# Letting an accumulating DMA make the lo part of every second weight chunk in the middle of a decoder layer's down projection

## The chip, the cores and the metric

The kernel runs on one core of one Trainium2 chip. Four engines compute: TensorE (PE in the profile; its weight loads are PEld), VectorE (DVE), ScalarE (ACT) and GpSimd (POOL). SyncE (SP) issues DMAs. Each engine works through its own queue in order and waits on semaphores for the others; transfers run on 16 DMA engines. The metric is the device time of one execution in microseconds, the median of several runs.

## The reference, cut to what matters

One decoder layer in float32, for 256 tokens of width 2048: a projection, two groups of attention heads, an output projection, a layer norm, a feed-forward block with a short convolution, and a second layer norm.

```python
D_MODEL = 2048; SEQ = 256; FFN_DIM = 5632
proj = h @ w_in[l]
a_out = diff_attention(q_d, k_d, v_d, lam, lam_init, subln_g[l], cos_d, sin_d)
b_out = moba_attention(q_m, k_m, v_m, cos_m, sin_m)
mix = jnp.concatenate([a_out, b_out], axis=-1) @ w_out[l]
h = layer_norm(DEEPNORM_ALPHA * h + mix, ln1_g[l], ln1_b[l])
f = conv_ffn(h, w_up[l], conv_w[l], conv_b[l], w_down[l])
h = layer_norm(DEEPNORM_ALPHA * h + f, ln2_g[l], ln2_b[l])

def conv_ffn(h, w_up, conv_w, conv_b, w_down):
    u = h @ w_up
    g, val = u[..., :FFN_DIM], u[..., FFN_DIM:]
    gp = jnp.pad(g, ((0, 0), (CONV_W - 1, 0), (0, 0)))
    gc = conv_b + sum(conv_w[j] * gp[:, j:j + S] for j in range(CONV_W))
    return (jax.nn.silu(gc) * val) @ w_down
```

The change lies in the last product, `(silu(gc) * val) @ w_down`, [256 tokens x 5632] by [5632 x 2048].

## The kernel before, in words

All weights pass through the core once, as a stream of chunks of 128 partitions x 2048 columns of float32 (1 MB): `v`, `q`, `k` chunks for the attention, 16 `o` chunks, 88 `g` and `u` chunks for the up projection, and 44 `d` chunks for the down projection, one for each 128 rows of `w_down`. In what follows a `d` chunk is counted from 0 to 43 (`i - first_d` in the code).

TensorE multiplies in a rounded format, float32r. To keep float32's precision, each operand is split into a hi part (the value rounded to float32r) and a lo part (the value minus hi, rounded too), and a product is made of three: hi by hi, hi by lo, lo by hi. `split(i, half)` does this for half a chunk: ScalarE copies 128 x 1024 columns of the loaded tile `raw` into `hi` (L122), and VectorE subtracts `hi` from `raw` into `lo` (L123). `hi` and `lo` come from a pool of six buffers each, that is three chunks; `raw` from a pool of four.

The program is written out step by step, one step for each chunk, and the order in which it is written is the order of every engine's queue. At the start of step i `begin(i)` puts down the split of the activations of chunk i + 2 (`split_act`, L447 on ScalarE and L448 on VectorE, in the down projection), the split of the second half of chunk i + 2, and the load of chunk i + 6 (L105, on SP's queue). In the middle of the step `middle(i)` puts down the split of the first half of chunk i + 3. So chunk i's load is put down six steps ahead, its first half is split 2.5 steps ahead and its second half two.

In the down projection the tokens stand still and the weights move. A step has 24 matmuls of 128 x 512 columns (`mm_d`, `mm_token`, L190): first columns 0 to 1023, for both halves of the tokens, then columns 1024 to 2047. For each pair of banks the order is hi by hi, twice, hi activations by lo weights, twice, lo activations by hi weights, twice. All eight PSUM banks accumulate over the 44 chunks; the last four chunks are taken out of the loop and finish bank by bank. At step 24 the second layer norm's two vectors are loaded (`load_gb`, L376, 1 MB each). After the last product z is normalised by VectorE, ScalarE and GpSimd and stored.

GpSimd does little: constants, a few powers, and the end of the last layer norm (L771, L772). All DMAs are issued by SP.

Tiles of the pool `keep` with the same tag share their place: tag `t2` holds x2 (the input), then h2 (the normed input of the up projection, in use until it ends), and from step 38 on `ends` (the split parts of the last four chunks).

Of the kernel before, what the change touches and what calls it, by code (L numbers as in the profile page):

```python
# [12 lines left out]
F32R = mybir.dt.float32r  # L13
AF = mybir.ActivationFunctionType
ALU = mybir.AluOpType

P = 128
# [15 lines left out]
LAM_INIT = 0.8 - 0.6 * math.exp(0.0)  # L33
MASKED = -3.0e38

# columns of the pack of per-partition vectors
C_G1, C_B1, C_W, C_CB, C_SG = 0, KT, 2 * KT, 2 * KT + 3 * FT, 2 * KT + 4 * FT
N_COLS = C_SG + 1

# [6 lines left out]
def hymba_layer(ctx: ExitStack, tc: tile.TileContext, a: dict):  # L46
# [13 lines left out]

    bank = [psum.tile([P, 512], F32, name=f"bank{i}") for i in range(8)]

    # ------------------------------------------------------------ weights
    loaded, parts = {}, {}

    stream = []
# [7 lines left out]
        for j in range(8):  # L74
            stream.append(("o", half, j, a["w_o"][half, j]))
    for f in range(FT):
        # the first two hold g and val of the first 128 features together, half of the rows each
        stream.append(("g", f, 0, a["w_u"][f, 0]))
        stream.append(("u", f, 0, a["w_u"][f, 1]))
    for f in range(FT):  # L80
# [4 lines left out]
    first_d = next(i for i, s in enumerate(stream) if s[0] == "d")  # L85

    def pieces(i, half=None):
        """Column ranges in which a chunk is loaded (or one half of it split): short where all else waits for it."""
        if i == 0:
            cuts = [0, 512, 1024, 1536, 2048]  # L90
        elif i < 4:
            cuts = [0, 512, 1024, 1536, 2048] if half is not None or i < 2 else [0, 1024, 2048]
        else:
            cuts = [0, 2048] if half is None else [0, 1024, 2048]
        both = [(x, y) for x, y in zip(cuts, cuts[1:])]
        return [p for p in both if half is None or p[0] // 1024 == half]

    def load(i):
        if i >= NS:
# [6 lines left out]
        loaded[i] = t  # L106

    def split(i, half, both=None):
        """hi and lo parts of half a chunk's columns, in the rotating buffers or in both."""
        if i >= NS or (i, half) in parts:  # L110
            return
        t = loaded[i] if half == 0 else loaded.pop(i)
        if both is None:
            hi = splits.tile([P, 1024], F32R, name="hi")
            lo = splits.tile([P, 1024], F32R, name="lo")
        else:
            hi, lo = both[:, half], both[:, 2 + half]
        for x, y in pieces(i, half):
            if i < 4 and x % 512 == 0:
                split_x(4 * i + x // 512, 4 * i + (y + 511) // 512)  # L120
            s = slice(x - 1024 * half, y - 1024 * half)
            ACT.activation(hi[:, s], t[:, x:y], AF.Copy)  # L122
            DVE.tensor_tensor(lo[:, s], t[:, x:y], hi[:, s].bitcast(F32), ALU.subtract)  # L123
        parts[i, half] = (hi, lo)

    def weights(i, x, w):
        """hi and lo parts of columns x to x + w of chunk i."""
        hi, lo = parts[i, x // 1024]
        return hi[:, x % 1024:x % 1024 + w], lo[:, x % 1024:x % 1024 + w]

    # ------------------------------------------------------------ activations of the layer's input
    # hi and lo parts of a row tile side by side, so that one product takes both
    x2 = keep.tile([P, KT, 2, S], F32R, name="x2", tag="t2")
    xh, xl = x2[:, :, 0], x2[:, :, 1]
    z = keep.tile([P, 2, D], F32, name="z")
# [7 lines left out]
        ACT.activation(xh[:, k0:k1], t, AF.Copy)  # L143
        DVE.tensor_tensor(xl[:, k0:k1], t, xh[:, k0:k1].bitcast(F32), ALU.subtract)

    # ------------------------------------------------------------ constants
    cst = {}

    def load_table(n):
# [21 lines left out]
    def lambdas():  # L171
        vec, lam4 = cst["vec"], cst["lam4"]
        pr = keep.tile([P, 2, SUB], F32, name="pr")
        DVE.tensor_tensor(pr[:, 0], lam4[:, 0], lam4[:, 1], ALU.mult)
        DVE.tensor_tensor(pr[:, 1], lam4[:, 2], lam4[:, 3], ALU.mult)
        ls = keep.tile([P, 4], F32, name="ls")
        DVE.reduce_sum(ls[:, 0:2], pr, axis=mybir.AxisListType.X)
        ACT.activation(ls[:, 2:4], ls[:, 0:2], AF.Exp)
        nlam = keep.tile([P, 2], F32, name="nlam")
        # -lambda = (exp(l2) - exp(l1)) - lambda_init  # L180
        DVE.tensor_tensor(nlam[:, 0:1], ls[:, 3:4], ls[:, 2:3], ALU.subtract)
        DVE.tensor_scalar(nlam[:, 1:2], nlam[:, 0:1], -LAM_INIT, None, op0=ALU.add)
        cst["nlam"] = nlam[:, 1:2]
        sg = keep.tile([P, 1], F32, name="sg")
        DVE.tensor_scalar(sg, vec[:, C_SG:C_SG + 1], 1.0 - LAM_INIT, None, op0=ALU.mult)
        cst["sg"] = sg

    # ------------------------------------------------------------ matrix products
    def mm(out, lhsT, rhs, start, stop):
        PE.matmul(out, lhsT, rhs, start=start, stop=stop)  # L190

    def mm_feature(dst, i, t2):
        """dst, a bank: [128 features, 256 tokens] twice, to be added up; the weights stand still."""
        for k in range(KT):
            if k == KT // 2:
                middle(i)
            wh, wl = weights(i, k * P, P)
            mm(dst, wh, t2[:, k].rearrange("p j t -> p (j t)"), k == 0, False)
            mm(dst[:, 0:S], wl, t2[:, k, 0], False, k == KT - 1)

    def added(dst, src):
        """dst = the sum of a bank's two halves."""
        ACT.activation(dst, src[:, S:2 * S], AF.Copy)
        DVE.tensor_tensor(dst, src[:, 0:S], dst, ALU.add)  # L204

    def mm_token(dst, i, x, ah, al, first, last):
        """dst, banks of [128 tokens, 512 features], from the chunk's columns x and on; the tokens stand still."""
        w = [weights(i, x + c * 512, 512) for c in range(len(dst))]
        for c, d in enumerate(dst):
            mm(d, ah, w[c][0], first, False)  # L210
        for c, d in enumerate(dst):
            mm(d, ah, w[c][1], False, False)
        for c, d in enumerate(dst):
            mm(d, al, w[c][0], False, last)

    # ------------------------------------------------------------ attention
    mh = keep.tile([P, NH, S], F32R, name="mh", tag="ma")
    ml = keep.tile([P, NH, S], F32R, name="ml", tag="mb")
    vals = {}
# [98 lines left out]
        att[h] = pt  # L318

    def mixed(h, scale):  # L320
        """hi and lo parts of a head's output, [head dim, tokens]."""
        scale = cst["sg"] if scale else None
        src = OB[:, S:2 * S]
        hi, lo = mh[:, h], ml[:, h]
        if scale is None:
            ACT.activation(hi, src, AF.Copy)
            DVE.tensor_tensor(lo, src, hi.bitcast(F32), ALU.subtract)
        else:
            ACT.activation(hi, src, AF.Copy, scale=scale)
            DVE.scalar_tensor_tensor(lo, src, scale, hi.bitcast(F32), op0=ALU.mult, op1=ALU.subtract)  # L330
# [34 lines left out]
        mm(OB[:, S:2 * S], v[:, 0, c], pt[:, 0:S], True, False)  # L365
        mm(OB[:, S + P:2 * S], v[:, 1, c], pt[:, S:S + P], False, True)

    # ------------------------------------------------------------ layer norm
    gb = {}
    stats = {}  # L370

# [20 lines left out]
        POOL.tensor_tensor(rstd, ve, cst["half"][:, 0:1], ALU.pow)  # L392
        return mv, rstd

    # ------------------------------------------------------------ feed-forward
    acts = {}

    def act_of(f):
# [21 lines left out]
    gates = {}  # L420

    def gated(f, g):
        """silu of the convolution; g [128 features, tokens]"""
        vec = cst["vec"]
        w = [vec[:, C_W + j * FT + f:C_W + j * FT + f + 1] for j in range(3)]
        gc = work.tile([P, S], F32, name="gc", tag="on")
# [21 lines left out]
        DVE.tensor_tensor(lo, src, hi.bitcast(F32), ALU.subtract)  # L448
        aparts[f] = (hi, lo)

    # ------------------------------------------------------------ the program
    idle = keep.tile([P, 512], mybir.dt.bfloat16, name="idle")
    DVE.memset(idle, 0.0)
    for i in range(4):
        load(i)
    for i in range(WARM):
        # the tensor engine's clock rises while the first loads are on their way
        mm(bank[7], idle[:, 0:P], idle, True, True)
    for i in range(2):
        split(i, 0)  # L460
# [2 lines left out]
    split(2, 0)  # L463

    def begin(i):
        """At the start of step i: what runs ahead of it, and what has waited for step i - 1."""
        urgent(i)
        j = i + 2
        if j < NS and stream[j][0] == "d":
            split_act(stream[j][1])  # L470
        split(j, 1)
        load(i + 6)
        pending(i)

    def middle(i):
        """Halfway through step i, when the first half of its weights is done with."""
        urgent(i + 0.5)
        if i + 3 < NS:
            split(i + 3, 0)
        pending(i + 0.5)  # L480
# [129 lines left out]
        DVE.tensor_tensor(hl[:, 4 * c:4 * c + 4, ts], hf, hi.bitcast(F32), ALU.subtract)  # L610

    def mm_first(t, c):
        """g and val of the first 128 features, [tokens, features], from a quarter of the rows."""
        ts = slice(t * P, (t + 1) * P)
        for kk in range(4):
            k = 4 * c + kk
# [81 lines left out]
    at(first_u + 3, act_out, 0, bank[0][:, S:2 * S])  # L698

    def h_piece(n):  # L700
        """z becomes the layer norm's own output, [tokens, features]."""
        t, c = divmod(n, 4)
        s = slice(c * 512, (c + 1) * 512)
        DVE.tensor_tensor(z[:, t, s], z[:, t, s], gb["g"][:, s], ALU.mult)
# [16 lines left out]
    def mm_d(i, t, cs):  # L721
        f = stream[i][1]
        ah, al = aparts[f]
        ts = slice(t * P, (t + 1) * P)
        # the last 512 columns of the second half of the tokens end in banks of their own
        end = FT - 1 - PAIRED_END if (t, cs) == (1, [3]) else FT - 1
        mm_token([bank[4 * t + c] for c in cs], i, cs[0] * 512, ah[:, ts], al[:, ts], f == 0, f == end)

    def mm_d_end(j):
        """The last chunks' share of half j of the last 512 columns, in a bank of its own."""  # L730
        for i in last:
            wh, wl = weights(i, 1536 + j * 256, 256)
            ah, al = (x[:, P:2 * P] for x in aparts[stream[i][1]])
# [91 lines left out]

# [1 line left out]
def _tables():  # L827
    """Rotary tables, [head dim, tokens], and the causal mask."""
    out = {}
    pos = np.arange(S, dtype=np.float32)  # L830
    for n, width, rot in (("d", SUB, SUB // 4), ("m", HD, HD // 4)):
# [61 lines left out]
```

## Time and profile before

| | |
|---|---|
| time, median of 3 runs | 1148.24 us (1147.97 to 1148.28) |
| span of the profiled execution | 1146.0 us |
| HBM read | 214.80 MB |
| DMA queues' share of 16 engines' span | 53.2% hardware_dynamic, 0.3% and 0.1% instruction |
| instructions | 15269 |

The span runs from the first to the last instruction of one profiled execution; the time of a run has a little more around it. In the page's rows of slices each digit is the busy share of one of 40 equal slices, in tenths. A grouped line reads: line, engine, operation, tiles out<-in, shapes, count | busy time, mean ns of one | idle time of the engine just before, and what ended it. A DMA row reads: tiles, issuing queue, count, KB each, median us from issue to landing.

### The profile page before, as it was taken

Reading aid. Unit: us, or ns where it says so; the run is one execution under the profiler, and the core shown is the slowest. Engines: PE = TensorE matmul, PEld = TensorE weight load, DVE = VectorE, ACT = ScalarE, POOL = GpSimd, SP = SyncE. Lnnn points to the kernel's source line nnn. Section 1 sums busy time; section 2 is a strip of 40 time slices with the busy share of each in tenths; the row PEclk is TensorE's granted clock in tenths of the full one; section 3 lists DMA queues with packets and bytes.
Section 4 is the critical chain, followed back from the end, with each engine's and each line's share of the span. In section 5 each row is a group of like instructions: output and inputs, shape, how many; then the busy total and the mean of one; then the engine's idle time right before and its main releaser. Section 6 shows DMA issues by size and latency. Waiting matters only on the chain.

```text
span 1146.0 us, 15269 instructions
## 1 busy us (share of the span) xinstructions
PE 1132.2 (99%) x5992; PEld 967.8 (84%) x5992; DVE 747.7 (65%) x1183; ACT 570.1 (50%) x895; POOL 20.8 (2%) x27
## 2 busy tenths in 40 slices
PE   9999999999999999999999999999999999999996
PEld 6888888888888898888888888888888888888885
DVE  6895886857745777777656666566666555555566
ACT  6555554544443485454554545455454444444441
POOL 0000000000000000000000000000000000000004
PEclk9999999999999999999999999999999999999998
DMA  9765455455455456555555555555555555556521
GB/s 329 280 220 193 153 179 179 154 182 184 156 178 190 174 219 222 184 187 190 194 201 185 184 188 187 200 193 188 184 184 193 195 192 191 184 210 233 185 106 74
DMA packets 33768, 217.89 MB, mean 190 GB/s; under 512 B 3744, under 2 KB 5664, under 8 KB 8480
## 3 DMA queue, kind: packets, MB, share of 16 engines
q1 hardware_dynamic: 33696, 216.92, 53.2%
q8 instruction: 47, 0.77, 0.3%
q14 instruction: 25, 0.20, 0.1%
HBM read 214.80 MB, written 2.10 MB: 189 GB/s over the span
## 4 chain that ended last, share of the span: by engine, by line
PE 98%; DVE 1%; POOL 1%; DMA 0%; ACT 0%; issue 0%; SPq 0%; POOLq 0%
PE bank L190 97%; PE bank L313 0%; POOL z L772 0%; DMA raw<-in_w_v 0%; POOL z L771 0%; DVE z L780 0%; PE bank L595 0%; PE bank L360 0%; ACT hf L598 0%; DVE h L610 0%; POOL rstd L392 0%; DVE z L822 0%; DVE bank L821 0%; DVE st L384 0%; DVE z L776 0%
## 5 line engine op out<-in xcount | busy, mean ns | idle before, releaser
L123 DVE TENSOR_TENSOR lo<-raw,hi 128x1024 fp32r<-128x1024 f32 (+1 forms) x394 | 468.0, 1202 | 283.8 <-ACT hi L122 283.4
L122 ACT ACTIVATE hi<-raw 128x1024 fp32r<-128x1024 f32 (+1 forms) x394 | 404.3, 1038 | 282.5 <-PE bank L190 252.4
L190 PE MATMUL bank<-h,hi 128*128 128x512 f32 x1376 | 477.2, 390 | 0.0
L190 PE MATMUL bank<-h,lo 128*128 128x256 f32 x1376 | 388.0, 282 | 0.0
L190 PEld LDWEIGHTS bank<-h,hi 128*128 128x128 f32 x1376 | 258.2, 188 | 54.1
L190 PEld LDWEIGHTS bank<-h,lo 128*128 128x128 f32 x1376 | 260.1, 189 | 0.0
L190 PE MATMUL bank<-x,hi 128*128 128x512 f32 x512 | 181.6, 396 | 0.0
L190 PE MATMUL bank<-x,lo 128*128 128x256 f32 x512 | 144.3, 282 | 0.0
L190 PEld LDWEIGHTS bank<-x,hi 128*128 128x128 f32 x512 | 96.1, 188 | 21.7 <-issue 1.3
L190 PE MATMUL bank<-hi,al 128*128 128x512 f32 (+1 forms) x338 | 107.1, 393 | 0.0
L190 PE MATMUL bank<-lo,ah 128*128 128x512 f32 (+1 forms) x338 | 107.1, 393 | 0.0
L190 PE MATMUL bank<-hi,ah 128*128 128x512 f32 (+1 forms) x338 | 107.1, 393 | 0.0
L190 PEld LDWEIGHTS bank<-x,lo 128*128 128x128 f32 x512 | 96.8, 189 | 0.2
L190 PE MATMUL bank<-hi,x 128*128 128x512 f32 x256 | 86.3, 407 | 0.4 <-ACT hi L122 0.4
L190 PEld LDWEIGHTS bank<-hi,al 128*128 128x128 f32 x338 | 63.7, 188 | 14.7
L190 PEld LDWEIGHTS bank<-lo,ah 128*128 128x128 f32 x338 | 63.7, 188 | 14.7
L190 PEld LDWEIGHTS bank<-hi,ah 128*128 128x128 f32 x338 | 63.6, 188 | 14.7
L190 PEld LDWEIGHTS bank<-hi,x 128*128 128x128 f32 x256 | 49.1, 192 | 13.0 <-ACT hi L122 1.3
L427 ACT ACTIVATE gc<-gs,vec 128x256 f32<-128x256 f32 x43 | 25.9, 602 | 58.7 <-DVE gs L204 58.7
L190 PE MATMUL bank<-lo,x 128*128 128x512 f32 x128 | 51.5, 402 | 0.0
L430 ACT ACTIVATE gc<-gc 128x256 f32<-128x256 f32 x44 | 18.4, 418 | 48.9 <-DVE gc L429 48.9
L447 ACT ACTIVATE ah<-act 128x256 fp32r<-128x256 f32 x44 | 18.2, 416 | 49.2 <-DVE lo L123 45.5
(122 smaller groups left out, 828.7 us busy)
## 6 DMA issues: line engine op xcount, KB each, us to landing
raw<-in_w_u SPq DMA_DIRECT2D x88, 1024.0 KB, 4.8
raw<-in_w_d SPq DMA_DIRECT2D x44, 1024.0 KB, 4.8
raw<-in_w_qk SPq DMA_DIRECT2D x32, 1024.0 KB, 4.9
raw<-in_w_o SPq DMA_DIRECT2D x16, 1024.0 KB, 4.8
raw<-in_w_v SPq DMA_DIRECT2D x12, 1024.0 KB, 4.8
raw<-in_w_v SPq DMA_DIRECT2D x8, 256.0 KB, 4.8
raw<-in_w_v SPq DMA_DIRECT2D x4, 512.0 KB, 7.9
z<-in_x SPq DMA_DIRECT2D x1, 2048.0 KB, 9.7
```

Of the source, the lines that this page charges most:

```text
L122: ACT.activation(hi[:, s], t[:, x:y], AF.Copy)
L123: DVE.tensor_tensor(lo[:, s], t[:, x:y], hi[:, s].bitcast(F32), ALU.subtract)
L190: PE.matmul(out, lhsT, rhs, start=start, stop=stop)
L427: ACT.activation(gc, g, AF.Identity, bias=vec[:, C_CB + f:C_CB + f + 1], scale=w[2])
L430: ACT.activation(gc, gc, AF.Silu)
L447: ACT.activation(hi, src, AF.Copy)
```

## The change

For the twelve `d` chunks 8, 10, ..., 30 the splitting is done in another way (`by_dma`, `split_dma`). For each half, ScalarE copies `raw` with scale -1 into lo, so that lo holds minus hi; a DMA from GpSimd's queue adds `raw` to lo in SBUF; and ScalarE copies `raw` into hi as before. VectorE has no part in it. hi and lo lie in one tile, `spare`, of the same place as h2 and `ends` (tag `t2`), with two slots that edited chunks use in turn; the rotating buffers are left to the odd chunks there. All of a chunk's four copies and two DMAs are put down in `begin`, three steps ahead of the chunk, after the second half of the chunk before it has been split and ahead of that step's load. The later calls of `split` for such a chunk find its parts made and return. The loading of `raw`, the matmuls and their order are as before. Comments were taken out of the file, and lines behind the new functions are numbered 18 to 20 higher.

```diff
+    def by_dma(i):
+
+        return first_d + 8 <= i < NS - 12 and (i - first_d) % 2 == 0
+
+    spare = []
+
+    def split_dma(i):
+        if not spare:
+            spare.append(keep.tile([P, 2, 2, 2048], F32R, name="spare", tag="t2"))
+        hi, lo = (spare[0][:, (i - first_d) // 2 % 2, j] for j in range(2))
+        t = loaded.pop(i)
+        for half in range(2):
+            s = slice(1024 * half, 1024 * (half + 1))
+            ACT.activation(lo[:, s], t[:, s], AF.Copy, scale=-1.0)
+            POOL.dma_start(lo[:, s], t[:, s], accum_op=ALU.add)
+            ACT.activation(hi[:, s], t[:, s], AF.Copy)
+            parts[i, half] = (hi[:, s], lo[:, s])
...
     def begin(i):
         urgent(i)
         j = i + 2
         if j < NS and stream[j][0] == "d":
             split_act(stream[j][1])
         split(j, 1)
+        if by_dma(i + 3):
+            split_dma(i + 3)
         load(i + 6)
         pending(i)
```

## The prediction

> **What bounds the kernel now.** I read the profile page first, for the engine that carries the span.
>
> ```profile
> PE 1132.2 (99%) x5992; PEld 967.8 (84%) x5992; DVE 747.7 (65%) x1183; ACT 570.1 (50%) x895; POOL 20.8 (2%) x27
> PE   9999999999999999999999999999999999999996
> PEclk9999999999999999999999999999999999999998
> PE 98%; DVE 1%; POOL 1%; DMA 0%; ACT 0%; issue 0%; SPq 0%; POOLq 0%
> ```
>
> TensorE is busy in every slice but the last, at full granted clock, and the chain that ended last is 98% matmuls. So VectorE at 65% is not a bound, only a helper that must be in time. The edit lies in the down projection, whose steps I marked off in the timeline by the split of the activations, the first ScalarE instruction of a step:
>
> ```profile
> 899.93 0.42 ACT L447 ACTIVATE ah<-act 128x256 fp32r<-128x256 f32 x1 [1.26 <-PE bank L190]
> ...
> 950.12 0.42 ACT L447 ACTIVATE ah<-act 128x256 fp32r<-128x256 f32 x1 [1.26 <-DVE lo L123]
> 950.59 1.06 ACT L122 ACTIVATE hi<-raw 128x1024 fp32r<-128x1024 f32 x1
> 953.38 1.06 ACT L122 ACTIVATE hi<-raw 128x1024 fp32r<-128x1024 f32 x1 [1.73 <-PE bank L190]
> ...
> 955.71 0.42 ACT L447 ACTIVATE ah<-act 128x256 fp32r<-128x256 f32 x1 [1.27 <-DVE lo L123]
> ```
>
> One step takes 5.58 us (955.71 - 950.12, and nine steps since 899.93), one matmul of its 24 so 0.232 us. The first row is the fifth of these splits, so it opens the step of chunk 2, and 950.12 that of chunk 11. The edited stretch, from three steps before chunk 8 to the end of chunk 30, then runs from about 917 to 1062. The windows and the grouped lines of 140 us of it:
>
> ```profile
> 922.00:1062.00 140.00, 140.00 (x604) 113.48 (x604) 72.14 (x76) 63.83 (x76) 0.00 (x0) 1.00 0.57 205
> L190 PE MATMUL bank<-hi,al 128*128 128x512 f32 x202 | 63.3, 394 | 0.0
> L123 DVE TENSOR_TENSOR lo<-raw,hi 128x1024 fp32r<-128x1024 f32 x51 | 62.5, 1225 | 55.6 <-ACT hi L122 55.6
> L122 ACT ACTIVATE hi<-raw 128x1024 fp32r<-128x1024 f32 x50 | 53.1, 1061 | 44.4 <-PE bank L190 43.2
> ```
>
> The columns of the first row are the busy time of PE, weight loads, VectorE, ScalarE and GpSimd, then clock, DMA share and GB/s. PE is busy in all 140 us and its matmuls have 0.0 us of idle time before them. ScalarE waits for matmuls to free buffers, VectorE waits for ScalarE: both are paced by PE. No wait here is left to remove. The resource that the edit newly loads is DMA, at 57%:
>
> ```profile
> DMA  4826646448256465382573643835649988357266
> GB/s 197 281 56 262 206 131 265 133 171 293 66 241 213 117 269 147 157 300 54 248 241 91 267 152 147 300 94 211 236 101 377 426 358 304 87 213 269 54 276 183
> q1 hardware_dynamic: 3920, 28.58, 56.8%
> raw<-in_w_d SPq DMA_DIRECT2D x25, 1024.0 KB, 4.8
> gb<-in_ln_g SPq DMA_DIRECT2D x1, 1024.0 KB, 6.9
> gb<-in_ln_b SPq DMA_DIRECT2D x1, 1024.0 KB, 9.0
> ```
>
> Loads come in bursts with gaps between them; only where the two layer-norm vectors are loaded too does it stay at nine tenths, there at up to 426 GB/s.
>
> **The change, part by part.**
>
> *VectorE.* 24 subtractions leave (12 chunks, two halves): 24 x 1.225 = 29.4 us off VectorE. Worth nothing, since none stands before PE (0.0 idle above). The gain is bounded above by the same zero.
>
> *ScalarE.* 24 copies with scale -1 are added, 24 x 1.061 = 25.5 us, priced as the hi copy of the same shape. ScalarE goes from 63.83 to about 89 of 140 us. They come in a burst: at the start of the step three before an edited chunk j it runs the activation split, hi of the odd chunk, then lo, hi, lo, hi: 0.42 + 5 x 1.06 = 5.7 us, against a step of 5.58. Queued behind is the next activation split, 0.15 us late and due two steps later. Cover: PE's own 5.58 us per step; the margin is some two steps. Cost zero. The edited chunks also leave the rotating hi and lo buffers, so odd chunks wait less for them; that helps nobody who bounds.
>
> *The wait for the spare buffers.* Chunk j overwrites the slot of chunk j - 4, whose last matmul ends just as that step starts. ScalarE is tied to that moment already by the activation split. Cost zero.
>
> *GpSimd.* It issues 24 DMAs and does nothing else in the window (0.00 busy). SP takes this much to issue one, and GpSimd's longest operation in the chain of waits was:
>
> ```profile
> L105 SPq DMA_DIRECT2D raw<-in_w_d x44: 327/328/328, 858.5 to 1097.9; - x44
> 1130.61 1.70 POOL z L771
> ```
>
> Between 0.33 and 1.70 us apiece; I take the longer one. Two issues in two steps (11.15 us) are then 3.4 us, hidden, and only add to the delay of the sum. Behind them on GpSimd's queue stands nothing until the last layer norm.
>
> *The raw buffers.* Until now a load waited for VectorE's subtraction; for the edited chunks it waits for both accumulating DMAs, and SP runs in order, so the odd chunk's load stands behind it.
>
> ```profile
> SPq L105 <- DVE lo L123: 556.7, 103, 25.2
> ```
>
> A load is issued 3.5 steps (19.5 us) before ScalarE's first copy of it and lands in 4.8, so 14.7 us of lateness are free. If the second accumulation, issued 4.7 us into a step, lands like a load, at 9.5, SP's next load goes out some 4 us late, inside that margin.
>
> *The accumulating DMA itself.* No row shows one. Deadlines first. The first lo half is ready for it at 0.42 + 2 x 1.06 = 2.5 us into the step, PE reads it three steps and two matmuls in, at 17.2 us: 14.7 us are allowed. The second is issued at 4.7 and read twelve matmuls later, at 20.0: 15.3 us. Behind a matmul that waits for lo stands all of PE. A whole load lands in 4.8, so a lone accumulation is in time. What matters is the throughput: in every two steps (11.15 us) there are two loads of 1 MB and two accumulations of 512 KB.
>
> Price of a load: 0.568 x 140 / 27.3 chunks of 1.05 MB (28.58 MB) = 2.91 us of all 16 engines in this stage; at the crowded rate, 1.05 MB / 426 GB/s = 2.46 us. One pass over 512 KB is half of it: 1.46 or 1.23 us. Lower bound of an accumulation: one pass, like a copy, 1.23 us. Upper bound: a row is read, added and written back with the time of two loads' landings one after the other, 9.6 us. The ends are far apart. I take three passes, since it fetches raw, fetches the destination and writes the destination, and I see no row that says that they overlap: 3 x 1.46 = 4.4 us, or 3 x 1.23 = 3.7 us at the crowded rate. That is nearest to the row of the 1 MB load of the same tile.
>
> *Sum.* At the stage's own price, two steps need 2 x 4.4 + 2 x 2.91 = 14.6 us of DMA in 11.15: 3.5 us too much, 12 times, 42 us; the two vector loads add 5; some 15 us of lateness are free: +32. At the crowded price, 2 x 3.7 + 2 x 2.46 = 12.3: 1.2 us too much, 14 us, +5 -15: +4. I take the middle, +18, rounded down to +17. On the profiled span, 1146.0 + 17 = 1163; with the 2.2 us that lie outside it (1148.24 - 1146.0), 1165 us.
>
> The collectives bear on this: the Trainium skill, "Collectives: The Full Stack", section "The bandwidth ceiling: the fold count and why AG ≠ RS ≠ AR", says that an add in the DMA path costs nothing itself and only doubles the reads. By it an accumulation would be two passes; no run here shows it. It is the first rival below.
>
> **The rivals.**
>
> *It fits (not slower).* The write-back runs beside the next row's reads, so an accumulation is two passes, 2 x 1.23 = 2.46 us. Two steps then need 4 x 2.46 = 9.8 us, less than 11.15. This case holds below (11.15 - 4.92) / 2 = 3.1 us per accumulation, with the free lateness (15 - 5) / 24 = 0.4 more, 3.5. For it: gaps in the DMA row, and landings with 15 us to spare. Against it: the loads leave gaps because they wait for buffers; they don't show that a read-modify-write streams. Time: 1148.2.
>
> *One at a time (much slower).* Accumulations wait for their own reads, the two landings of 4.8 us, while loads pass between them. A pair takes 19.2 us, 8.05 more than two steps; 12 x 8.05 - 15 = +82: 1230. For it: 256 KB and 1 MB loads land alike, so much of a landing is waiting and not bytes; against it: bursts at 426 GB/s show many packets in flight at once.
>
> ```profile
> raw<-in_w_v SPq DMA_DIRECT2D x8, 256.0 KB, 4.8
> ```
>
> *Faster.* Something I can't see paces matmuls by VectorE's traffic; idle 0.0 and clock 1.00 in the window speak against it. If the 24 subtractions' whole 29.4 us slowed PE by a tenth, it would be -3: 1145.
>
> **How the numbers follow.** Overfilled DMA 50%, own range 1152 to 1180. It fits, 23%. One at a time 17%. Other costs, such as descriptor making on GpSimd longer than 5.6 us apiece or instruction fetches behind crowded queues, 6%, slower. Faster, 4%. A measurement of this kernel tells about 0.2% (2.3 us) from no change. Faster 0.04, same 0.23, slower 0.73. The range from 1147.6 to 1215 holds the fit, the forecast and about half of the slow rival.
>
> **What would show it.** Right: in the edited stretch the DMA row stands at nine tenths throughout, PE gets gaps before matmuls that read the spare tile's lo, released by the accumulating DMA, growing after some four pairs; the window of 140 us becomes about 157, all else keeps its length; VectorE loses 24 instructions, ScalarE gains 24. Wrong: PE keeps 0.0 idle and DMA stays below nine tenths (it fits); or DMA has gaps while PE waits for the accumulation (one at a time); or PE waits for ScalarE's hi, which would void my zero for the burst; or GpSimd's queue is solid with issues.

## The result, and the profile after

The changed kernel takes 1148.99 us (median of 20 runs, 1147.57 to 1150.36) against 1147.57 us of the kernel before on the same chips (20 runs, 1146.48 to 1148.29): a ratio of 1.0014, 95% interval 1.0007 to 1.0020. That is 1.4 us more, within the 0.2% that the prediction called no change. The forecast was 17 us more.

From the page of the changed kernel, the lines that answer to those of before (the lines have moved: L123 is now L141, L190 L208, L105 L123; L111 to L113 are the new copies and the new DMA):

```profile
span 1146.8 us, 15285 instructions
PE 1132.4 (99%) x5992; PEld 967.0 (84%) x5992; DVE 717.6 (63%) x1159; ACT 587.1 (51%) x919; POOL 41.9 (4%) x51
DVE  6895886857745777776666666566666523232566
POOL 0000000000000000000000000000000011110004
DMA  9755455455455456555555555555555589999721
q1 hardware_dynamic: 33696, 216.92, 53.0%
q0 software_dynamic: 3456, 12.58, 5.8%
```

The edit does what it says: VectorE has lost 24 instructions and 30 us, ScalarE has gained 24 instructions, GpSimd has 24 more and shows in four slices where it had nothing. DMA goes from five and six tenths to eight and nine there. TensorE's busy time is the same within 0.2 us.

The windows, the grouped lines and the DMA answer for the same 140 us as before, then the waits of SP's queue over the whole edited stretch (917 to 1062), of the changed kernel:

```profile
922.00:1062.00 140.00, 140.00 (x602) 113.16 (x601) 41.97 (x51) 78.06 (x97) 19.43 (x23) 1.00 0.99 279
L208 PE MATMUL bank<-spare,ah 128*128 128x512 f32 x192 | 52.7, 396 | 0.0
L112 POOL DMA_DIRECT2D spare<-raw x23 | 20.0, 869 | 105.8 <-ACT spare L111 104.7 <-PE bank L208 1.0
...
q1 hardware_dynamic: 3625, 26.42, 51.8%
q0 software_dynamic: 3456, 12.58, 47.1%
raw<-in_w_d SPq DMA_DIRECT2D x24, 1024.0 KB, 9.1
spare<-raw POOLq DMA_DIRECT2D x23, 512.0 KB, 9.5
...
SPq L123 <- DMA spare<-raw: 124.5, 12, 16.3
```

TensorE is busy in all 140 us, and the matmuls that read the accumulated lo have 0.0 us of idle time before them, as before the change. Yet the DMA share went from 0.57 to 0.99, and both kinds of transfer now land 9 to 10 us after their issue. All of the new work fits, by this share only just. Does the backlog grow from pair to pair? Two windows of 22 us (about four steps) of the DMA answer, one early and one with the two layer-norm vectors:

```profile
DMA  8997999989999999999999998999999999999986
GB/s 164 223 231 127 223 201 186 134 104 141 365 343 417 432 417 432 432 402 417 387 432 432 417 402 313 298 283 268 290 298 328 238 246 216 201 201 216 216 171 119
q0 software_dynamic: 562, 2.04, 51.0%
q1 hardware_dynamic: 576, 4.19, 48.9%
raw<-in_w_d SPq DMA_DIRECT2D x4, 1024.0 KB, 8.5
spare<-raw POOLq DMA_DIRECT2D x4, 512.0 KB, 8.6
```

```profile
q1 hardware_dynamic: 676, 5.01, 60.4%
q0 software_dynamic: 514, 1.84, 42.7%
raw<-in_w_d SPq DMA_DIRECT2D x4, 1024.0 KB, 17.1
spare<-raw POOLq DMA_DIRECT2D x4, 512.0 KB, 9.7
gb<-in_ln_g SPq DMA_DIRECT2D x1, 1024.0 KB, 11.2
gb<-in_ln_b SPq DMA_DIRECT2D x1, 1024.0 KB, 13.0
```

The first is 966 to 988: four loads (4.19 MB) and four accumulations land, in 8.5 and 8.6 us. The second is 1032 to 1054: only there do the loads fall behind, to 17.1 us, and they catch up when the edit ends. There is no growth in between (9.3 and 9.5 us for 988 to 1010, 9.1 and 9.4 for 1010 to 1032). Nor does the time shrink that is left between an accumulation's landing and TensorE's first read of it. By the trace it is 4.7 us for the first half of chunk 8, 3.7 for that of chunk 26, and 2.6 at the least up to chunk 28; only for the last one, behind the vectors' loads, is it 0.9 us.

The row of rates in the first window shows two levels. Where accumulations run alone (201 to 216 GB/s, near its end) 512 KB take some 2.5 us, and where loads run alone (417 to 432 GB/s, in its middle) 1 MB takes some 2.5 us too.

So the mechanism to be settled is the price of an accumulation, the time for which it holds all 16 engines. Three theories stood before the experiments: two passes (it fits), three passes (the prediction's, covered for some reason), and one pass (the 0.99 only counts packets that wait). A second question is where the remaining 1.4 us come from.

### The profile page after: what moved, and what is told of

Read it like the earlier page. It is cut to its first block, busy times and chain, and to the rows that moved or that the text cites. A ratio compares the mean times of both kernels' runs of the same rounds, so it can differ in the third digit from the quotient of the medians.

```text
span 1146.8 us, 15285 instructions
## 1 busy us (share of the span) xinstructions
PE 1132.4 (99%) x5992; PEld 967.0 (84%) x5992; DVE 717.6 (63%) x1159; ACT 587.1 (51%) x919; POOL 41.9 (4%) x51
## 3 DMA queue, kind: packets, MB, share of 16 engines
q0 software_dynamic: 3456, 12.58, 5.8%
## 4 chain that ended last, share of the span: by engine, by line
PE 96%; DVE 2%; DMA 1%; SPq 0%; ACT 0%; POOL 0%; issue 0%; POOLq 0%
PE bank L208 95%; DMA raw<-in_w_v 1%; PE bank L331 0%; DVE st L402 0%; DVE z L399 0%; DVE z L800 0%; PE bank L615 0%; SPq L157 0%; DVE z L796 0%; PE bank L378 0%; SPq L123 0%; POOL rstd L410 0%; ACT hf L618 0%; DVE h L630 0%; DVE z L842 0%
## 5 line engine op out<-in xcount | busy, mean ns | idle before, releaser
L141 DVE TENSOR_TENSOR lo<-raw,hi 128x1024 fp32r<-128x1024 f32 (+1 forms) x370 | 438.5, 1200 | 249.0 <-ACT hi L140 248.3
L140 ACT ACTIVATE hi<-raw 128x1024 fp32r<-128x1024 f32 (+1 forms) x370 | 378.5, 1036 | 246.5 <-PE bank L208 207.6
L208 PE MATMUL bank<-h,hi 128*128 128x512 f32 x1376 | 477.2, 390 | 0.0
L208 PE MATMUL bank<-h,lo 128*128 128x256 f32 x1376 | 388.1, 282 | 0.0
L208 PEld LDWEIGHTS bank<-h,hi 128*128 128x128 f32 x1376 | 258.3, 188 | 53.9
L208 PEld LDWEIGHTS bank<-h,lo 128*128 128x128 f32 x1376 | 260.6, 189 | 0.0
L208 PE MATMUL bank<-x,hi 128*128 128x512 f32 x512 | 181.6, 396 | 0.0
L208 PE MATMUL bank<-x,lo 128*128 128x256 f32 x512 | 144.3, 282 | 0.0
L208 PEld LDWEIGHTS bank<-x,hi 128*128 128x128 f32 x512 | 96.2, 188 | 21.6 <-issue 1.3
L208 PEld LDWEIGHTS bank<-x,lo 128*128 128x128 f32 x512 | 96.9, 189 | 0.2
L208 PE MATMUL bank<-hi,x 128*128 128x512 f32 x256 | 85.6, 404 | 0.2 <-ACT hi L140 0.2
L208 PE MATMUL bank<-lo,ah 128*128 128x512 f32 (+1 forms) x242 | 77.2, 394 | 0.0
L208 PE MATMUL bank<-hi,ah 128*128 128x512 f32 (+1 forms) x242 | 77.0, 393 | 0.0
L208 PE MATMUL bank<-hi,al 128*128 128x512 f32 (+1 forms) x242 | 76.9, 392 | 0.0
L466 DVE TENSOR_TENSOR al<-act,ah 128x256 fp32r<-128x256 f32 x44 | 18.6, 424 | 87.2 <-PE bank L208 66.0
L208 PEld LDWEIGHTS bank<-hi,x 128*128 128x128 f32 x256 | 48.3, 189 | 13.1 <-ACT hi L140 2.0
L208 PEld LDWEIGHTS bank<-hi,al 128*128 128x128 f32 x242 | 45.6, 188 | 10.6
L208 PEld LDWEIGHTS bank<-lo,ah 128*128 128x128 f32 x242 | 45.7, 189 | 10.5
L208 PEld LDWEIGHTS bank<-hi,ah 128*128 128x128 f32 x242 | 45.5, 188 | 10.5
L208 PE MATMUL bank<-spare,ah 128*128 128x512 f32 x192 | 52.7, 396 | 0.0
L208 PE MATMUL bank<-lo,x 128*128 128x512 f32 x128 | 51.2, 400 | 0.7 <-DVE lo L141 0.7
```

## The experiments

All kernels below are the changed kernel with one edit, but for the last, which starts from the kernel before. The first four ran on one chip beside the kernel before (1147.57 us there), the others on another (1147.73 us).

### The changed kernel once more

> The changed kernel once more, unaltered. All theories: median 1 to 2 us above the kernel before; in the profile the stretch from the activation split at the start of chunk 5's step to that of chunk 31 takes about 145.46 us (145.00 before), DMA is busy 0.97 to 1.00 of it, and PE has no idle time there.

1148.66 us, ratio 1.0011 (1.0002 to 1.0020). The time repeats. That TensorE would have no idle time is a miss: the list of waits has two for an accumulating DMA, for the last one, behind the vectors' loads.

```profile
PE bank L208 <- DMA spare<-raw: 0.2, 1, 0.2
PEld bank L208 <- DMA spare<-raw: 0.6, 1, 0.6
```

The columns are total, times and longest, in us. With that the changed kernel is at the edge: in one profiled execution no matmul waits, in another one does, for 0.6 us.

### The edit without its DMA

```diff
         ACT.activation(lo[:, s], t[:, s], AF.Copy, scale=-1.0)
-        POOL.dma_start(lo[:, s], t[:, s], accum_op=ALU.add)
         ACT.activation(hi[:, s], t[:, s], AF.Copy)
+        DVE.tensor_tensor(lo[:, s], t[:, s], hi[:, s].bitcast(F32), ALU.subtract)
```

> VectorE makes lo as before the change (raw minus hi), but all else of the edit stays: the copies with scale -1, the spare tile, the place three steps ahead. No accumulating DMA. If DMA traffic slows TensorE's pace (theory A): the stretch goes back to 145.0 us and the median to that of the kernel before, within 0.5 us. If the schedule or the spare tile does it (theory B): the stretch stays at 145.4 to 145.5 and the median 1 to 2 us above. DMA share back to 0.54 to 0.57 under both.

1147.69 us, ratio 1.0004 (0.9996 to 1.0013). Its DMA share is 0.57 again. The step starts tell more than the median. Here are, from the timelines, the activation splits that open the steps of chunks 5 and 33, of the kernel before, the changed kernel and this one, each in a fence of its own:

```profile
916.67 0.42 ACT L447 ACTIVATE ah<-act 128x256 fp32r<-128x256 f32 x1 [1.27 <-DVE lo L123]
1072.83 0.42 ACT L447 ACTIVATE ah<-act 128x256 fp32r<-128x256 f32 x1 [1.27 <-DVE lo L123]
```

```profile
916.76 0.42 ACT L465 ACTIVATE ah<-act 128x256 fp32r<-128x256 f32 x1 [1.27 <-DVE lo L141]
1073.38 0.42 ACT L465 ACTIVATE ah<-act 128x256 fp32r<-128x256 f32 x1 [1.26 <-DVE lo L141]
```

```profile
915.87 0.42 ACT L465 ACTIVATE ah<-act 128x256 fp32r<-128x256 f32 x1 [1.27 <-DVE lo L141]
1072.49 0.42 ACT L465 ACTIVATE ah<-act 128x256 fp32r<-128x256 f32 x1 [1.26 <-DVE lo L141]
```

28 steps take 156.16 us before the change, 156.62 after it, and 156.62 without its DMA (up to chunk 31, the stretch named beforehand, 145.00, 145.46 and 145.46). So 0.46 us of slower pace has nothing to do with DMA; my theory A for the pace falls. The median, 1.0 us under the changed kernel's on the same chip, suggests that the DMA has a part in the rest, but the intervals of the two ratios overlap, and theory B's 1 to 2 us did not come.

### A plain copy in place of the addition

```diff
-        POOL.dma_start(lo[:, s], t[:, s], accum_op=ALU.add)
+        POOL.dma_start(lo[:, s].bitcast(F32), t[:, s])
```

> The same DMA without the addition: a plain copy of raw into lo, the same bytes in the same place on the same queue (lo is then raw itself, so the output is not the reference's). If an accumulation costs two passes (theory A: two reads, the write beside them), the copy takes half the DMA time: the software queue's share of the window 922 to 1062 falls from 47% to about 24%, and it lands in 5 to 7 us instead of 9.5. If three passes (my prediction): to about 16%. If the addition and second read are free: it stays at 47%. Time: within 0.2% of the kernel before under all.

The DMA answer for 922 to 1062:

```profile
q1 hardware_dynamic: 3857, 28.06, 58.2%
q0 software_dynamic: 3456, 12.58, 22.1%
raw<-in_w_d SPq DMA_DIRECT2D x25, 1024.0 KB, 7.1
spare<-raw POOLq DMA_DIRECT2D x22, 512.0 KB, 8.8
```

The same 3456 packets and 12.58 MB hold the 16 engines for 22.1% of the time instead of 47.1%: 0.221 x 140 / 24 = 1.29 us for a copy, 0.471 x 140 / 24 = 2.75 us for an accumulation, 2.1 times as much. That is theory A's halving; three passes would have left 16%. The waiting of packets on each other doesn't make this factor: among the single packets in the traces, one of 4 KB takes 328 ns in the median as an accumulation, in the changed kernel and in the doubled one below alike, and 159 ns as a copy; one of 8 KB takes 309 ns as a load. With 128 packets over 16 engines that is 2.62 us for an accumulation, 1.27 for a copy and 2.47 for a load. The copy's landings at 8.8 us are a miss: I expected 5 to 7, and halving the work hardly made them quicker. The time is 1148.69 us, ratio 1.0010 (1.0000 to 1.0019), the same as with the addition.

### Each accumulation twice

```diff
             parts[i, half] = (hi[:, s], lo[:, s])
+        to = acts[2][:, 12:16].rearrange("p k t -> p (k t)")
+        POOL.dma_start(to, t[:, 0:1024], accum_op=ALU.add)
+        to = tables[0][:, 0:4].rearrange("p k t -> p (k t)")
+        POOL.dma_start(to, t[:, 1024:2048], accum_op=ALU.add)
```

The scratch places are four unused rows of the last `act` tile and the attention's tables, which are put into one tile for it.

> Each accumulating DMA twice: a second one of the same size adds raw to a scratch place that nothing reads (so four per two steps instead of two). Theory A (2.46 us of all 16 engines each, DMA now nearly full): two steps need 4 x 2.46 + 4.92 = 14.8 us in 11.15, 12 times 3.6 = 44, +5 -15: 30 to 40 us slower, PE waiting for the accumulating DMAs and the loads. Prediction's three passes (3.7 us): 4 x 3.7 + 4.9 = 19.7, 90 to 100 us slower. If the 0.99 DMA share is only packets waiting and an accumulation costs one pass (1.23 us): 9.8 us in 11.15, nothing, under 3 us slower.

1193.51 us, 45.9 more (ratio 1.0404, 1.0385 to 1.0423, from two runs). Windows and DMA of 922 to 1062, and TensorE's waits of 922 to 1080:

```profile
922.00:1062.00 140.00, 123.87 (x486) 95.44 (x484) 31.56 (x40) 61.32 (x77) 33.71 (x39) 0.94 1.04 265
...
q0 software_dynamic: 5314, 19.40, 71.9%
q1 hardware_dynamic: 2426, 17.65, 32.2%
...
PEld bank L215 <- DMA spare<-raw: 22.6, 14, 3.0
PE bank L215 <- DMA spare<-raw: 16.5, 11, 2.6
```

Here is the picture that the prediction had drawn for the change itself: TensorE idle 16 of 140 us, waiting for the accumulated lo, and DMA full. One pass is out; it would have cost nothing. An accumulation again holds the engines for 0.719 x 140 / 37 = 2.72 us (19.40 MB are 37 half chunks). With 2.75 us and a load's 2.69 (0.489 x 22 / 4, from the window of 966 to 988 above), the sum would be 4 x 2.75 + 2 x 2.69 = 16.4 us in 11.15: 12 x 5.2 + 5 - 15 = 53. That window has the lowest price of a load; the four windows from 944 to 1032 give 2.90 in the mean, and the sum 58. Measured 46: more than the 30 to 40 of theory A with its 2.46 us, and half of what three passes give.

### One accumulation more per pair

Only the first of the two added DMAs.

> Only the first half of each edited chunk is added a second time into scratch: three accumulations per two steps. At the 2.75 us that the traces show for one and 2.69 us for a load: 3 x 2.75 + 2 x 2.69 = 13.6 us in 11.15, 12 x 2.5 = 30, +5 -15: about 20 us slower (15 to 25). At the prediction's 3.7 us: 3 x 3.7 + 4.9 = 16.0, about 48 slower. If only the depth of the queue counted and the fourth transfer of the doubled run did the harm: under 3 us.

1169.81 us, 22.1 more (ratio 1.0193, 1.0174 to 1.0212, from two runs), as expected from 2.75 us. TensorE waits 17.4 us for weight loads from the spare tile and 14.1 us for matmuls, overlapping lists of the same seven delays. The third accumulation alone takes DMA from "fits" to 22 us. The fourth adds 23.9, or 2.0 us for each of the 12, but the first pairs are among these, which wait for nothing yet. What a further one costs where TensorE does wait is read from its first matmuls on the spare tile for chunks 14 and 30, eight pairs apart, with three accumulations a pair and then with four:

```profile
967.22 1.09 PE L213 MATMUL bank<-spare,ah 128*128 128x512 f32 x4
1069.96 0.63 PE L213 MATMUL bank<-spare,ah 128*128 128x512 f32 x2
```

```profile
967.39 0.63 PE L215 MATMUL bank<-spare,ah 128*128 128x512 f32 x2
1092.37 0.63 PE L215 MATMUL bank<-spare,ah 128*128 128x512 f32 x2
```

A pair takes 12.84 and 15.62 us, so the fourth accumulation costs 2.8 us, near the 2.62 of its median packets and the 2.75 of its share. (The added ones also hold `raw` longer, so that loads start later. That this costs something besides was not tested apart; by their shares, 1.02 and 1.04 for 939 to 1061, the engines were full in both.)

### Sixteen chunks instead of twelve

```diff
-        return first_d + 8 <= i < NS - 12 and (i - first_d) % 2 == 0
+        return first_d + 4 <= i < NS - 8 and (i - first_d) % 2 == 0
```

> Sixteen edited chunks (4, 6, ..., 34) instead of twelve. Theory A (two steps need 2 x 2.75 + 2 x 2.69 = 10.9 us of DMA in 11.15, it keeps up): no growth, accumulations land in 9 to 10 us throughout but for the vector loads, PE waits under 2 us in all, the median within 1 us of the changed kernel's. Rival (it is overfilled and the free lateness of 15 us covered it only because twelve chunks were few): landings grow and PE waits 3 us or more.

1150.38 us, ratio 1.0024 (1.0014 to 1.0033). From the DMA answer for 1010 to 1032, the last window before the vectors land, and from the list of TensorE's waits:

```profile
raw<-in_w_d SPq DMA_DIRECT2D x4, 1024.0 KB, 8.8
spare<-raw POOLq DMA_DIRECT2D x5, 512.0 KB, 8.9
...
PEld bank L208 <- DMA spare<-raw: 1.4, 1, 1.4
```

By 1032 some 24 accumulations have been issued (since about 894, two every 11.15 us), as many as the changed kernel has in all, and the landings are 8.8 and 8.9 us: no backlog has grown, and the overfill theory falls. TensorE waits once, 1.4 us for a weight load (1.0 us for its matmul), behind the vectors' loads, where the edit is still running. Its excess of 2.65 us is 1.2 to 1.6 above the changed kernel's, a little over my bound of 1 us.

### The vectors' loads put off

```diff
-        if i == first_d + 24:
+        if i == first_d + 34:
             load_gb(2, keep.tile([P, 2, D], F32, name="gb2", tag="ma"))
```

> The changed kernel with the two layer-norm vectors (2 MB) loaded at step 34 instead of 24, behind the edited stretch. Theory A (DMA is filled to some 98% and only these two loads push it over, for a moment): no wait of PE for the accumulating DMA anywhere, the weight loads from 1032 to 1054 land in 9 to 10 us and not 17, and the median is that of the run without DMA, 1147.3 to 1148.1 us. Rival (the rest of the 1 us comes with any DMA from GpSimd's queue): the median stays at 1148.4 to 1149.

TensorE waits for nothing, the weight loads of 1032 to 1054 land in 9.3 us instead of 17.1, and the last accumulation in 10.4 us instead of 13.8. So these loads are what pushes DMA to its edge, as theory A has it. (The 28 steps take 156.62 us, as in the changed kernel's own profile; in its repetition, with its waits, they take 157.04.) The median does not follow: 1148.42 us, ratio 1.0008 (0.9998 to 1.0017), inside the rival's bounds and not inside A's. Part of that is pace (0.46 us). For another part the traces bear the rival out. From the landing of the last store to the end of the span, 1.06 us pass in the kernel before, without the DMA and with the spare tile alone, but 1.26 or 1.27 us in every kernel with DMAs from GpSimd's queue, the plain copy too (1.76 in the doubled one). Outside the span, the median over all runs is 1.75 to 1.81 us without such DMAs and 1.98 to 2.10 us with them (1.86 in the doubled one). Together that is some 0.4 us; by which mechanism stays open.

### The spare tile alone

The kernel before; `split` puts the parts of chunks 8, 10, ..., 30 into the spare tile at their old times.

```diff
-        if both is None:
+        if by_dma(i):
+            if not spare:
+                spare.append(keep.tile([P, 2, 2, 2048], F32R, name="spare", tag="t2"))
+            slot = spare[0][:, (i - first_d) // 2 % 2]
+            hi, lo = (slot[:, x, 1024 * half:1024 * (half + 1)] for x in range(2))
+        elif both is None:
```

> The kernel before, but the parts of chunks 8, 10, ..., 30 are put into the spare tile, by ScalarE and VectorE at their old times; no copies with scale -1, no DMA, no earlier place. The stretch from the split at chunk 5's step to that at chunk 33's takes 156.16 us in the kernel before and 156.62 both with and without the DMA. If where hi and lo lie sets TensorE's pace: 156.6. If the earlier place or ScalarE's load does: 156.2.

The two splits, from its timeline:

```profile
916.90 0.42 ACT L470 ACTIVATE ah<-act 128x256 fp32r<-128x256 f32 x1 [1.27 <-DVE lo L146]
1073.52 0.42 ACT L470 ACTIVATE ah<-act 128x256 fp32r<-128x256 f32 x1 [1.26 <-DVE lo L146]
```

156.62 us again: no DMA, no new copies, no earlier place, only other addresses for hi and lo. And only the steps of the edited chunks are longer: that of chunk 8 takes 5.61 us (933.63 to 939.24), that of chunk 9 takes 5.58 (to 944.82). The 0.46 us are shown to come with the spare tile, 38 ns for each of the twelve chunks. (The time, of a single run, is 1148.45 us.)

## Why the prediction was wrong

*What failed.* The step "I take three passes, since it fetches raw, fetches the destination and writes the destination, and I see no row that says that they overlap". The mechanism of the sum was right, and this term of it was too large: 3.7 to 4.4 us, measured 2.75 by the share of its packets, 2.62 by their median, 2.8 by what a further one adds. An accumulation holds the engines for 2.1 copies; that fits a write that runs beside two reads, though no trace shows the passes singly. With two passes in place of three, either of the prediction's prices gives no loss: 4 x 2.46 = 9.8 us, or 2 x 2.91 + 2 x 2.91 = 11.7, whose 6 us of excess and 5 of the vectors are within the 15 free. The forecast put the point from which it decides at 3.1 us per accumulation, and the truth lies just below it; the added third accumulation, at 22.1 us where the sum with 2.75 gives 20 to 25 (for loads of 2.69 and 2.90 us), shows that the point is real.

How full DMA is, no sum says exactly. By median packets two steps need 2 x 2.62 + 2 x 2.47 = 10.2 us of the 11.2 that they take; by shares 2 x 2.75 + 2 x 2.90 = 11.3, and there packets that wait on each other are counted. That it fits is shown by the landings, by what is left before TensorE's reads, and by the sixteen chunks.

*The rival that came true* is "It fits", with its two passes and its 1148.2 us; it had 23%. The rule quoted there from the Trainium skill ("Collectives: The Full Stack", "The bandwidth ceiling: the fold count and why AG ≠ RS ≠ AR") spoke for it, and the trace agrees: 47.1% against the copy's 22.1% of the engines' time, a factor of 2.1 where the rule gives 2. The Trainium skill tells it of rings of several ranks, not of a transfer inside one SBUF, and it was the nearest evidence there was; I gave more weight to the lack of a row.

*"One at a time"* foresaw landings of 9.6 us, and 9.5 came, but they were not taken one at a time: the first two, for one, are issued at 919.6 and 921.4 and land at 929.5 and 931.9, and every pair was in time.

*The steps priced at zero* held. VectorE's 30 us bought nothing. ScalarE's burst delays nobody: TensorE has no wait for it. (ScalarE is busy 78.06 us of the 140 and not 89: two of the 24 new copies fall ahead of the window, and copies that follow each other closely overlap in the records. Nothing hung on it.) An issue holds GpSimd for 0.87 us, between the bounds of 0.33 and 1.70. SP stands at the new wait 12 times, 16.3 us at the longest and 124.5 in all, where it stood 133.5 us for VectorE's subtractions in the same stretch before: a wait changed its owner.

*The free lateness* of 15 us was not used up by an excess that grew from pair to pair, as the sum supposed. What used it is the landing of each accumulation under load, and most of all the vectors' loads: the longest, 13.8 us, is that of the last accumulation, issued at 1045.5, which TensorE reads at 1060.2. From the tile's own answer:

```profile
L112 POOL DMA_DIRECT2D spare<-raw x24: 860/869/1042, 919.6 to 1045.5; - x24
DMA to landing us min/median/max: 4.8/9.6/13.8
```

*The sign that misled.* I named "the DMA row stands at nine tenths throughout" as a mark of overfilling. It came true without TensorE losing anything. The share counts the time that packets are under way, and those that wait on each other count too (it reads 1.04 in the doubled kernel, more than the engines have); what tells is whether landings grow.

*The 1.4 us that are there* (0.8 to 2.3 by the interval): 0.46 us is the spare tile's place (shown). Some 0.4 us come at the end of the span and outside it, in every kernel with DMAs from GpSimd's queue; their mechanism stays open. Waits behind the vectors' loads come in some executions: they lengthen the 28 steps by 0.42 us in the repetition's profile and by nothing in the changed kernel's first one. The rest is within the interval.

## What to carry to other kernels

Moving work off an engine that nobody waits for wins nothing; the question is only whether the place it goes to has room, and that is a sum per period: transfers, times their engine time, against the steps' length. Price a read-modify-write DMA in SBUF at about two copies of its size, and check the deadline of each by its landing under load, not alone. When a resource is nearly full, look for the one-off transfer that falls into the same stretch, and move that.

## What the runs showed of the hardware that was not expected

The pace of matmuls depends a little on where their moving operand lies: with nothing else changed, 28 steps took 156.62 us with twelve chunks in the spare tile and 156.16 with all in the rotating buffers.

A copy of half the DMA work doesn't land in half the time: 8.8 us against 9.5, at a DMA share of 0.81 against 0.99.

An accumulating DMA in SBUF holds the engines for about two copies of its size: 2.75 us against 1.29 for 512 KB, and 328 ns against 159 for the median packet.

When TensorE begins to wait, its granted clock falls: 1.00 in the window of the changed kernel, 0.94 in that of the doubled one. Matmuls behind a wait are then slower there, as two rows of four matmuls each show, the first 1.6 us after the end of a wait of 1.82 us (at 985.40), the second 6.2 us after it:

```profile
986.98 1.91 PE L215 MATMUL bank<-spare,ah 128*128 128x512 f32 x4
991.63 1.10 PE L215 MATMUL bank<-spare,ah 128*128 128x512 f32 x4
```

DMA was full there, so whether the slower matmuls added to the 46 us is not shown.
